# A two-layer trunk on one core: layer 0's first half of the stream kept in SBUF between the MLP and layer 1, mixer weights split 1024 columns at a time

## The chip, the cores and the metric

The kernel runs on one core of a Trainium2 chip. The number that counts is the device time of one execution in microseconds. The core has five engines that each work through their own list of instructions in order, and wait for one another by semaphores: TensorE (PE in the profile; its weight loads are shown apart as PEld), VectorE (DVE), ScalarE (ACT), GpSimd (POOL) and SyncE (SP). SyncE does no arithmetic here: it issues DMA transfers. GpSimd issues some too.

## The reference

The model is a trunk of two residual layers on a stream `x` of 1024 tokens by 1024 features, in float32, with 256 memory tokens beside it.

```python
for layer in range(DEPTH):                       # 2
    h = rms_norm(x, norm_mix[layer])
    if layer == 0:
        y_mix, xq = rglru_group(h, w_in_a, ...)  # gated linear recurrence
    else:
        y_mix, xq = fox_group(h, w_in_b, ...)    # causal attention, 8 heads
    y_mem = memory_group(xq, mem, ...)           # 4 heads onto the memory
    x = x + concatenate([y_mix, y_mem]) @ w_out[layer]
    h = rms_norm(x, norm_mlp[layer])
    x = x + square(relu(h @ w_mlp_in[layer])) @ w_mlp_out[layer]
```

`rms_norm` divides each token by the root of its mean square, so each norm needs sums of squares over all 1024 features of a token. `memory_group` projects the normalised memory tokens by `w_mem_kv` to keys and values, and attends to them with the query `xq`, which comes from the projection of the stream.

## The kernel before

**Layout.** The stream lies transposed, features on partitions: eight feature tiles `k` of 128, in two token halves `h` of 512. A tile 128x512 is 256 KB. Between the stages the stream lives in DRAM, in the array `xspill` (`self.xs`); tiles of it are loaded by `load_x` (L538) into buffers `f`.

**Three matmuls for a product.** Every float32 operand is split into a rounded part and a remainder (`wh` and `wl` for weights, two buffers `r` for activations), and a product is three matmuls: `wh` with both parts of the activation, `wl` with the first. For a weight chunk, `_wpart` (L317 to L320) does this: ScalarE casts (`wh<-wr`, L319), VectorE or GpSimd subtracts (`wl<-wr,wh`, L320). Which engine subtracts a piece is read from `self.pool_parts`, set from the table `TUNE` by stage. A plan of all weight chunks in the order of use says for each in how many pieces it is split; `wr` is loaded by SyncE (L315), three buffers each of `wh` and `wl` go round for most stages, and the next chunks are split as the buffers come free. Chunks that are needed twice are written to DRAM after the split (L343) and loaded back.

**The passage from layer 0's MLP to layer 1.** The MLP runs over eight groups of hidden features (`mlp`). In each, `mlp_z` makes the hidden tiles and `mlp_out` multiplies them by the second weight; both use a scheme of seven products for two token halves and two feature halves, so one product's result is used in two places. In `mlp_out`, `first` copies a product from PSUM (ScalarE, L1075), `then` adds a second product (VectorE, L1080), and `send` (L1220) has GpSimd's queue add the tile to `xspill` by an accumulating DMA. `kv` projects the memory for layer 1: eight weight chunks (`wkv`), taken in pairs, each with 12 matmuls 128x256 into each of two PSUM tiles (L388). In step with it runs `norm_split_back`: for each of the eight feature tiles of the first half it reloads the tile (L538), splits it (ScalarE L488, VectorE L491), squares it (ScalarE L441) and adds the squares up (VectorE L447). Then `xq_proj` multiplies these tiles by `wxqb`.

**The order.** Generators are advanced in a written order; `weave(main, side, rate)` advances the side `rate` steps for each step of the main one. A scheduler with its own time model then orders each engine's list, so the list can differ from the code's order.

**The start.** In layer 0 the tokens are also loaded in a token-major copy (`xtok`), whose squares ScalarE sums (`tok_sums`, L476). `norm_fin_g` makes the reciprocal roots, and where a broadcast over partitions is wanted, GpSimd puts them on a diagonal (L530) and a matmul with ones spreads them (L381, `pso<-f,ones`). For later norms the squares of tiles are summed over partitions by matmuls 128x1 with a constant column (`sq_pe`, `sq_mm`, L465).

## Time and profile before

| | |
|---|---|
| time, median of 3 runs | 2108.54 us (2106.35 to 2111.91) |
| profiled execution, its own time | 2108.65 us |
| its span, first to last instruction | 2106.9 us |
| mean granted TensorE clock | 0.988 |
| TensorE busy | 2055.2 us, 10378 instructions |
| VectorE, ScalarE, GpSimd busy | 1564.0, 1154.3, 463.3 us |
| reloads of `xspill` by SyncE (L538 and others) | 88 of 256 KB |
| accumulating writes to `xspill` by GpSimd | 240 of 256 KB |

A row such as `L320 DVE TENSOR_TENSOR wl<-wr,wh 128x1024 ... x222 | 273.3, 1231 | 172.5 <-ACT wh L319 171.7` reads: line of the kernel, engine, operation, output from inputs, tile shape, count; then busy microseconds and nanoseconds of one; then the microseconds that the engine idled just before these instructions, and what released it. Line numbers are those of the kernel before; in the changed one they are 1 to 23 higher. In a row of waits stand the engine and the line that waited, what it waited for, and the total, the number and the longest of the waits. SPq is SyncE's own queue. Slices of the span are 52.7 us.

### The profile page before, as it was taken

What the parts mean: (1) busy time and instruction counts of PE and PEld (TensorE: products, weight loads), DVE (VectorE), ACT (ScalarE), POOL (GpSimd) and SP (SyncE); (2) the same over time, 40 slices, a digit from 0 to 9 for tenths busy, and PEclk for the clock granted to TensorE, in tenths of its full rate; (3) what the DMA queues carried; (4) which work ended last, traced back from release to release, by engine and by line L of the source; (5) the groups of instructions that cost most, each with busy time, mean ns of one, the idle gap of its engine ahead of it and who ended that gap; (6) DMA issues with size and microseconds to landing.
All of it is one profiled execution on the core that took longest, in us unless ns stands there. A gap on an engine that the chain in (4) does not pass through costs nothing. (4 is left out here: it accounts for less than half of the span.)

```text
span 2106.9 us, 29666 instructions
## 1 busy us (share of the span) xinstructions
PE 2055.2 (98%) x10378; PEld 1712.8 (81%) x10378; DVE 1564.0 (74%) x2916; ACT 1154.3 (55%) x2172; POOL 463.3 (22%) x590
## 2 busy tenths in 40 slices
PE   9999999999999999997999999999999999999999
PEld 7987788888788888876998998777778888888887
DVE  8878698776776776785585778787787768658757
ACT  7756656554554554555464655576554555445544
POOL 1132210201201201214252333232012122022021
PEclk9999999999999999998899999999999999999999
DMA  7433362635635635748568437743446674365374
GB/s 276 151 99 117 101 195 76 130 81 110 131 81 110 135 77 109 160 94 246 192 232 295 151 100 267 239 149 117 145 101 140 139 179 95 80 147 99 78 184 120
DMA packets 122646, 301.56 MB, mean 143 GB/s; under 512 B 13760, under 2 KB 15872, under 8 KB 122496
## 3 DMA queue, kind: packets, MB, share of 16 engines
q1 hardware_dynamic: 79584, 209.41, 29.6%
q0 software_dynamic: 42912, 90.26, 22.8%
q8 instruction: 81, 1.33, 0.3%
q14 instruction: 69, 0.57, 0.1%
HBM read 190.46 MB, written 109.15 MB: 142 GB/s over the span
## 5 line engine op out<-in xcount | busy, mean ns | idle before, releaser
L1064 PE MATMUL pspt<-r,wh 128*128 128x512 f32 x1536 | 491.6, 396 | 1.0 <-ACT wh L319 1.0
L320 DVE TENSOR_TENSOR wl<-wr,wh 128x1024 fp32r<-128x1024 f32 (+2 forms) x354 | 337.9, 965 | 198.0 <-ACT wh L319 196.9
L319 ACT ACTIVATE wh<-wr 128x1024 fp32r<-128x1024 f32 (+3 forms) x403 | 304.5, 777 | 296.4 <-PE pss L1064 73.2
L1220 POOL DMA_DIRECT2D xspill<-f x240 | 212.1, 1111 | 854.8 <-DVE f L1080 825.1
L1064 PEld LDWEIGHTS pspt<-r,wh 128*128 128x128 f32 x1536 | 288.3, 188 | 71.5 <-ACT wh L319 1.4
L1064 PE MATMUL pss<-r,wh 128*128 128x512 f32 x1024 | 329.1, 396 | 0.4 <-DVE r L499 0.4
L1064 PE MATMUL pspt<-r,wl 128*128 128x512 f32 x768 | 304.0, 396 | 0.0
L1064 PE MATMUL pspj<-r,wh 128*128 128x512 f32 x832 | 272.1, 399 | 1.0 <-DVE r L491 1.0
L388 PE MATMUL pspj<-wh,r 128*128 128x256 f32 (+1 forms) x1280 | 252.5, 290 | 15.3 <-ACT r L488 11.7
L499 DVE TENSOR_TENSOR r<-f,r 128x512 fp32r<-128x512 f32 x282 | 191.0, 696 | 75.9 <-DMA xspill<-f 61.3
L1064 PEld LDWEIGHTS pss<-r,wh 128*128 128x128 f32 x1024 | 192.1, 188 | 48.5 <-DVE r L499 0.8
L388 PEld LDWEIGHTS pspj<-wh,r 128*128 128x128 f32 x1280 | 207.1, 194 | 19.7 <-ACT r L488 13.0
L496 ACT ACTIVATE r<-f 128x512 fp32r<-128x512 f32 x282 | 169.6, 625 | 82.8 <-DMA xspill<-f 25.1
L1064 PE MATMUL pss<-r,wl 128*128 128x512 f32 x512 | 202.4, 395 | 0.0
L1064 PEld LDWEIGHTS pspj<-r,wh 128*128 128x128 f32 x832 | 156.6, 189 | 39.8 <-DVE r L491 1.8
L388 PE MATMUL pspj<-wl,r 128*128 128x256 f32 (+1 forms) x640 | 184.9, 289 | 0.2 <-POOL wl L320 0.2
L1064 PEld LDWEIGHTS pspt<-r,wl 128*128 128x128 f32 x768 | 144.5, 188 | 35.2
L1064 PE MATMUL pspj<-r,wl 128*128 128x512 f32 x416 | 164.9, 397 | 0.0
L388 PE MATMUL pspj<-r,wh 128*128 128x512 f32 x480 | 157.8, 404 | 3.9 <-DVE wr L836 1.7
L1085 ACT ACTIVATE f<-f 128x512 f32<-128x512 f32 x128 | 78.8, 626 | 105.1 <-DVE f L1084 102.8
L388 PEld LDWEIGHTS pspj<-wl,r 128*128 128x128 f32 x640 | 123.7, 193 | 1.2 <-POOL wl L320 0.4
L1064 PEld LDWEIGHTS pss<-r,wl 128*128 128x128 f32 x512 | 96.2, 188 | 23.8 <-issue 0.5
(301 smaller groups left out, 3570.2 us busy)
## 6 DMA issues: line engine op xcount, KB each, us to landing
wr<-in_w_dram SPq DMA_DIRECT2D x136, 512.0 KB, 3.9
xspill<-f POOLq DMA_DIRECT2D x240, 256.0 KB, 7.2
f<-xspill SPq DMA_DIRECT2D x88, 256.0 KB, 4.6
xspill<-f SPq DMA_DIRECT2D x48, 256.0 KB, 3.1
wsp<-wh SPq DMA_DIRECT2D x22, 512.0 KB, 5.7
wsp<-wl SPq DMA_DIRECT2D x22, 512.0 KB, 6.1
wh<-wsp POOLq DMA_DIRECT2D x21, 512.0 KB, 5.2
wl<-wsp POOLq DMA_DIRECT2D x21, 512.0 KB, 5.4
```

The lines of the kernel that those rows point to most:

```text
L319: self.wact = self.nc.scalar.activation(hi, raw, AF.Copy)
L320: eng.tensor_tensor(lo, raw, hi.bitcast(F32), ALU.subtract)
L388: self.lastmm = self.nc.tensor.matmul(out, lhsT=a, rhs=b, start=(j == 0), stop=(j == n - 1))
L496: i = self.nc.scalar.activation(hi[:, :n], src, AF.Copy)
L499: self.nc.vector.tensor_tensor(lo[:, :n], src, hi[:, :n].bitcast(F32), ALU.subtract)
L1064: self.lastmm = self.nc.tensor.matmul(ps, lhsT=a, rhs=b, start=(start and c == 0 and j == 0), stop=(c == n - 1 and j == 2), skip_group_che ...
L1085: self.lastsq = self.nc.scalar.activation(f[:, n], f[:, n], AF.Square)
L1220: nc.gpsimd.dma_start(self.xs[2 * q + a, :, b * H:(b + 1) * H], f[:, n], accum_op=ALU.add)
```

## The change

It has five parts.

1. The lists of pieces for GpSimd in `TUNE` are emptied: every weight remainder is VectorE's.
2. The mixer's chunks (`plan_kv`, `plan_mv`, `plan_fox`) are split in one piece of 1024 (or 1056) columns, where it was four. That concerns 41 chunks, of which the first chunk of all keeps its four pieces.
3. The 128x1 matmuls that sum squares before the MLP are taken up later, from hooks in the MLP's first group, and their PSUM bank is taken when the first is done.
4. At the start, `tok_sums` issues all its loads at once; the sums of the second token half stand at the head of `in_g0` and their `norm_fin` at its third step.
5. In layer 0's last MLP group, the first half's eight stream tiles are loaded while the hidden tiles are made. The products for them are added to these tiles on VectorE, the first one too. They are written to `xspill` by plain DMAs of SyncE, and `norm_split_back` takes them from SBUF.

```diff
--- before.py
+++ after.py
@@ -165,11 +165,11 @@
     "cp_kv0": 1,
     "cp_kv1": 0,
     "pa": (),
-    "pb0": (1, 3),
-    "pb1": (0, 1, 2, 3),
-    "pb2": (3,),
+    "pb0": (),
+    "pb1": (),
+    "pb2": (),
     "pm0": (),
-    "pm1": (1, 3),
+    "pm1": (),
 }
 
 
@@ -218,6 +218,7 @@
         self.parked = {}
         self.stp = {}
         self.tst = {}
+        self.xres = {}
         self.xg = [None, None]
         self.ymix = [None, None]
         self.hs = [None, None]
@@ -453,11 +454,12 @@
         if behind is not None:
             self.after(i, behind)
         if m == 0:
-            self.stp[h] = self.psum("o"), []
+            self.stp[h] = [None, []]
         self.stp[h][1].append((m, sq))
-        self.sq_mm(h, 2)
 
     def sq_mm(self, h, keep):
+        if self.stp[h][0] is None:
+            self.stp[h][0] = self.psum("o")
         st, todo = self.stp[h]
         while len(todo) > keep:
             m, sq = todo.pop(0)
@@ -469,15 +471,17 @@
     def tok_sums(self, src, n, tag, behind=None):
         nc = self.nc
         st = self.small(2 * n, tag, 1)
+        xs = [self.F.get() for _ in range(2 * n)]
+        for k, x in enumerate(xs):
+            nc.sync.dma_start(x[:, :H], src[k // 2, :, k % 2 * H:(k % 2 + 1) * H])
         for t in range(n):
             for j in range(2):
-                x = self.F.get()
-                nc.sync.dma_start(x[:, :H], src[t, :, j * H:(j + 1) * H])
+                x = xs[2 * t + j]
                 i = nc.scalar.activation(x[:, :H], x[:, :H], AF.Square, scale=1.0 / math.sqrt(D),
                                          accum_out=st[:, j * n + t:j * n + t + 1])
                 if behind is not None:
                     self.after(i, behind)
-                self.F.put(x)
+        self.F.put(*xs)
         return st
 
     def tok_var(self, v, st, n):
@@ -538,7 +542,7 @@
         self.nc.sync.dma_start(x[:, :H], src[k, :, h * H:(h + 1) * H])
         return x
 
-    def norm_split(self, h, g, src, stats, tok=None):
+    def norm_split(self, h, g, src, stats):
         xs = self.xg[h] = []
         for k in range(8):
             x = self.load_x(k, h, src)
@@ -547,14 +551,12 @@
             xs.append(self.split(x[:, :H], self.pc(g, k)))
             self.F.put(x)
             yield
-        if tok is not None:
-            self.tst[h] = self.tok_sums(tok[4 * h:4 * h + 4], 4, f"tst{h}", self.last_hi)
-
-    def norm_split_back(self, h, g, src):
+
+    def norm_split_back(self, h, g):
         nc = self.nc
         xs = self.xg[h] = [None] * 8
         for j, k in enumerate((0, 2, 4, 6, 1, 3, 5, 7)):
-            x = self.load_x(k, h, src)
+            x = self.xres.pop(k)
             xs[k] = self.split(x[:, :H], self.pc(g, k), behind=self.wact)
             self.sqacc(j, h, x[:, :H], nc.vector, self.last_hi)
             self.F.put(x)
@@ -605,7 +607,7 @@
 
     def plan_kv(self, l, idx=range(8)):
         for c in idx:
-            self.plan.append(self.ent("wkv", l * 8 + c, 1024, 4))
+            self.plan.append(self.ent("wkv", l * 8 + c, 1024, 1))
 
     def kv(self, l):
         nc = self.nc
@@ -792,7 +794,7 @@
 
     def plan_mv(self, name, idx=range(4)):
         for i in idx:
-            self.plan.append(self.ent(name, i, 1024, 4))
+            self.plan.append(self.ent(name, i, 1024, 1))
 
     def proj_T(self, xs, tag="pj"):
         wh, wl = self.wnext()
@@ -1226,7 +1228,20 @@
             nc.sync.dma_start(self.out[2 * q + a, :, b * H:(b + 1) * H], f[:, n])
             self.F.put(f)
 
+        def held(a):
+            def first(q, ps):
+                self.plus(self.xres[2 * q + a], ps)
+
+            def then(q, ps):
+                x = self.xres[2 * q + a]
+                self.plus(x, ps)
+                nc.sync.dma_start(self.xs[2 * q + a, :, :H], x[:, n])
+
+            return first, then
+
         def keep(a, b):
+            if b == 0 and self.xres:
+                return held(a)
             dst = []
 
             def first(q, ps):
@@ -1274,19 +1289,25 @@
         def hook0(key):
             if key in ahead:
                 self.xsplit(ahead[key])
+            if key in ("b11", "b21"):
+                self.sq_mm(1, 6 if key == "b11" else 3)
             if key in ("t2", "t3"):
                 advance(nf)
 
         def hook7(key):
             if key == "t2" and nxt is not None:
                 advance(nxt)
+            if key == "t1" and not l:
+                self.xres = {m: self.load_x(m, 0, self.xs) for m in (0, 2, 4, 6, 1, 3, 5, 7)}
             if key == "t1" and l:
                 self.acc = [self.load_x(2 * q, 0, self.xs) for q in range(4)]
 
         for p in wait:
             for k in ("t3", "t1"):
                 self.xsplit(k)
+            self.sq_mm(1, 5)
             drain(p)
+            self.sq_mm(1, 2)
         for g in range(8):
             if g == 0 and g in self.parked:
                 for k in ("t3", "t1"):
@@ -1326,7 +1347,7 @@
         for w in ("wkb", "wqb"):
             self.plan_mv(w, (2 * c, 2 * c + 1))
         for kk in range(2):
-            self.plan.append(self.ent(f"wvb{c}", kk, 1024 if c else 1056, 4))
+            self.plan.append(self.ent(f"wvb{c}", kk, 1024 if c else 1056, 1))
 
     def fox_proj(self, h, c):
         nc = self.nc
@@ -1591,7 +1612,7 @@
 
 
         xk = self.ins["xtok"]
-        nrm = [self.norm_split_first(0, "gmix0", xT, xk), self.norm_split(1, "gmix0", xT, False, xk)]
+        nrm = [self.norm_split_first(0, "gmix0", xT, xk), self.norm_split(1, "gmix0", xT, False)]
         advance(nrm[0])
         kv = self.kv(0)
 
@@ -1623,7 +1644,10 @@
                     yield
 
         def in_g0():
+            self.tst[1] = self.tok_sums(xk[4:], 4, "tst1", self.wact)
             for m in range(4):
+                if m == 2:
+                    self.norm_fin(1, True)
                 for _ in range(4):
                     advance(kv)
                     yield
@@ -1656,7 +1680,6 @@
         weave(self.xq_proj(0), lru0, TUNE["xq0"])
         drain(lru0)
         self.xg_free(0)
-        self.norm_fin(1, True)
         xa0 = self.xattn(0)
         weave(self.xq_proj(1), xa0, TUNE["xq1"])
         weave(in_u1(), xa0, TUNE["in_u1"])
@@ -1679,8 +1702,8 @@
 
 
         self.fox_setup()
-        advance(kv, 6)
-        weave(kv, self.norm_split_back(0, "gmix1", self.xs), 1.0)
+        advance(kv, 2)
+        weave(kv, self.norm_split_back(0, "gmix1"), 1.0)
         self.vst = {}
         xq = self.xq_proj(0, 1)
         advance(xq, 4)
```

Counted over the whole kernel: remainders of 1024 columns on VectorE go from 222 to 261 (and 2 of 1056), of 256 columns from 112 to 4; on GpSimd 49 remainders go. ScalarE has 38 more casts of 1024 columns (and 2 of 1056), 152 fewer of 256 and 8 fewer of 264, and 8 fewer PSUM copies; VectorE 8 more additions from PSUM. GpSimd issues 232 accumulating DMAs in place of 240, SyncE 56 plain writes to `xspill` in place of 48. The number of matmuls is the same, 10280.

SyncE at the passage from layer 0's MLP to layer 1, where `wxqb` and `wkb` are weights of layer 1's mixer, and `f_...<-xspill` are the first half's stream tiles. Before:

```order
L315 DMA wr_69<-in_wxqb_dram 128x1024
L538 DMA f_894_8484<-xspill 128x512
L315 DMA wr_70<-in_wxqb_dram 128x1024
L538 DMA f_899_8509<-xspill 128x512
L315 DMA wr_71<-in_wxqb_dram 128x1024
L315 DMA wr_72<-in_wxqb_dram 128x1024
L538 DMA f_907_8573<-xspill 128x512
L343 DMA wsp_100<-wh_75 128x1024
L343 DMA wsp_101<-wl_78 128x1024
L315 DMA wr_69<-in_wkb_dram 128x1024
L343 DMA wsp_102<-wh_73 128x1024
L538 DMA f_911_8596<-xspill 128x512
```

With the change, the loads of the tiles, in the list just ahead of the last MLP weights (`w`) and the first of `wkv`:

```order
L542 DMA f_831_7771<-xspill 128x512
L542 DMA f_832_7773<-xspill 128x512
L542 DMA f_833_7775<-xspill 128x512
L542 DMA f_834_7777<-xspill 128x512
L542 DMA f_835_7779<-xspill 128x512
L542 DMA f_836_7781<-xspill 128x512
L542 DMA f_837_7783<-xspill 128x512
L316 DMA wr_69<-in_w_dram 128x1024
L316 DMA wr_71<-in_w_dram 128x1024
L316 DMA wr_72<-in_w_dram 128x1024
L316 DMA wr_70<-in_w_dram 128x1024
L316 DMA wr_69<-in_wkv_dram 128x1024
```

The reloads stood between the weights of the two projections of layer 1; now they stand in a row, ahead of the last four MLP chunks, and in the place of the reloads there are none.

TensorE in the keys and values of layer 1 (`kv`), where a first chunk is `wh_73`, `wl_76`, the second of the pair `wh_74`, `wl_77`, and `pspt` a PSUM tile. Before, at the end of a first chunk:

```order
L388 MATMUL pspt_8670<-wl_76,r_862_8137 128x256
L388 MATMUL pspt_8670<-wh_73,r_863_8138 128x256
L388 MATMUL pspt_8670<-wh_74,r_872_8186 128x256
L388 MATMUL pspt_8670<-wl_77,r_872_8186 128x256
L388 MATMUL pspt_8670<-wh_74,r_873_8187 128x256
L388 MATMUL pspt_8670<-wh_74,r_872_8186 128x256
```

With the change, likewise:

```order
L389 MATMUL pspt_8521<-wl_76,r_862_8049 128x256
L389 MATMUL pspt_8521<-wh_73,r_863_8050 128x256
L389 MATMUL pspt_8521<-wh_74,r_872_8098 128x256
L389 MATMUL pspt_8548<-wh_73,r_856_8001 128x256
L389 MATMUL pspt_8548<-wl_76,r_856_8001 128x256
L389 MATMUL pspt_8548<-wh_73,r_857_8002 128x256
```

and at the end of that chunk's matmuls for the second PSUM tile:

```order
L389 MATMUL pspt_8548<-wh_73,r_862_8049 128x256
L389 MATMUL pspt_8548<-wl_76,r_862_8049 128x256
L389 MATMUL pspt_8548<-wh_73,r_863_8050 128x256
L389 MATMUL pspt_8548<-wh_74,r_872_8098 128x256
L389 MATMUL pspt_8521<-wl_77,r_872_8098 128x256
L389 MATMUL pspt_8521<-wh_74,r_873_8099 128x256
```

Before, the remainder of the second chunk is used by the 14th matmul of a PSUM tile. With the change a second PSUM tile is begun in between, so that it is used by the 27th of the pair.

TensorE at the broadcast of the second token half's roots in layer 0 (`f_...,ones`). Before, it stands in the first query projection (PSUM tiles `pspj` of 128x256):

```order
L388 MATMUL pspj_1929<-wh_75,r_110_1008 128x256
L388 MATMUL pspj_1929<-wl_78,r_110_1008 128x256
L388 MATMUL pspj_1929<-wh_75,r_111_1009 128x256
L381 MATMUL pso_1551<-f_157_1546,ones 128x512
L388 MATMUL pspj_1929<-wh_75,r_113_1071 128x256
L388 MATMUL pspj_1929<-wl_78,r_113_1071 128x256
```

With the change:

```order
L389 MATMUL pspj_1080<-r_11_171,wh_73 128x512
L389 MATMUL pspj_1080<-r_10_170,wl_76 128x512
L382 MATMUL pso_857<-f_105_852,ones 128x512
L389 MATMUL pspj_1080<-r_13_177,wh_73 128x512
L389 MATMUL pspj_1080<-r_14_178,wh_73 128x512
L389 MATMUL pspj_1080<-r_13_177,wl_76 128x512
```

It now stands some 390 matmuls earlier, in the gate projection (128x512).

## The prediction

> **What bounds the kernel now.** I read the page's shares first, then its 40 slices, then the stretch where the slices dip, as a table of windows.
>
> ```profile
> PE 2055.2 (98%) x10378; PEld 1712.8 (81%) x10378; DVE 1564.0 (74%) x2916; ACT 1154.3 (55%) x2172; POOL 463.3 (22%) x590
> PE   9999999999999999997999999999999999999999
> PEclk9999999999999999998899999999999999999999
> ```
>
> TensorE is busy for 98% of the span of 2106.9 us; VectorE for 74%, ScalarE for 55%. Taking work from ScalarE or GpSimd as such is therefore worth nothing: only time in which TensorE idles, or runs at a lower clock, can be won. Slices 18 and 19 (each 52.7 us, so about 950 to 1050) are the only two with a dip in both rows. That is the passage from layer 0's MLP to layer 1's mixer:
>
> ```profile
> 917.50:956.60 39.10, 38.72 (x166) 30.90 (x165) 32.37 (x53) 25.49 (x50) 16.00 (x19) 1.00 0.67 143
> 956.60:983.30 26.70, 24.51 (x199) 23.50 (x198) 17.31 (x37) 16.22 (x45) 13.91 (x16) 1.00 0.83 240
> 983.30:1010.50 27.20, 12.71 (x52) 10.43 (x52) 11.14 (x21) 10.07 (x21) 3.31 (x3) 0.55 0.55 199
> 1010.50:1017.00 6.50, 6.50 (x32) 6.50 (x32) 2.57 (x14) 1.27 (x4) 0.00 (x0) 0.51 0.01 3
> ```
>
> (Columns: stretch, length, then busy time and instructions of PE, PEld, DVE, ACT and POOL, the granted clock, DMA share.) The first is the MLP's end, the second the memory K and V projection of layer 1, in which TensorE loses 2.2 us. In the third, where the memory query projection needs the normalised stream, it is busy 12.71 of 27.20 us for only 52 matmuls, at clock 0.55; in the fourth it is busy throughout, at 0.51. What it waits for stands in the waits from 950 to 1060 (total us, times, longest) and in SyncE's queue from 930 to 1012:
>
> ```profile
> PE pspj L388 <- ACT r L488: 11.7, 4, 5.4
> PE pspt L675 <- DVE r L668: 2.6, 1, 2.6
> ACT r L488 <- DMA f<-xspill: 23.1, 7, 7.1
> SPq L538 <- DVE f L447: 21.9, 5, 7.9
> SPq L538 <- DMA xspill<-f: 8.9, 1, 8.9
> ```
>
> Read backwards: TensorE waits for the cast of a stream tile (L488), the cast waits for the tile's reload from DRAM (seven times, 23.1 us), and the reload on SyncE waits once for the MLP's last accumulating write to land (8.9 us) and five times for the square-add (L447) of an earlier tile, whose buffer it takes. The reloads are a serial loop, one buffer per turn.
>
> **The change part by part.** *Kept tiles (the main term).* The eight reloads and their waits leave that loop: the tiles are fetched during the MLP's last group, get the products added in SBUF, and are there when the projection of K and V begins. At full pace the second stretch does 199 matmuls in 24.51 us, 0.123 us each. By that rate the 52 matmuls of the third take 6.4 us, not 27.2: 20.8 to gain. The fourth at full clock takes 0.51 × 6.50 = 3.3 us: 3.2 to gain. With the 2.2 idle us of the second this is 26.2 us at most.
>
> What is late next is the eight tiles' splitting. These are the durations:
>
> ```profile
> L488 ACT ACTIVATE r<-f,par 128x512 fp32r<-128x512 f32 x56 | 39.7, 717 | 51.0 <-DMA f<-xspill 40.9 <-DVE r L491 4.0 <-DMA f<-in_xT_dram 3.1
> L491 DVE SCALAR_TENSOR_TENSOR r<-f,par,r 128x512 fp32r<-128x512 f32 x56 | 42.6, 764 | 33.9 <-ACT r L488 29.7 <-ACT wh L319 4.0
> L447 DVE TENSOR_TENSOR f<-f,f 128x512 f32<-128x512 f32 x21 | 14.7, 701 | 1.0 <-ACT f L441 0.5 <-DVE fsm L1469 0.4
> L320 DVE TENSOR_TENSOR wl<-wr,wh 128x1024 fp32r<-128x1024 f32 x222 | 273.3, 1231 | 172.5 <-ACT wh L319 171.7 <-issue 0.3
> L319 ACT ACTIVATE wh<-wr 128x1024 fp32r<-128x1024 f32 x223 | 236.1, 1059 | 274.5 <-PE pss L1064 71.7 <-DMA wr<-in_w_dram 67.0 <-PE pspt L1064 53.6
> L1080 DVE TENSOR_TENSOR f<-f,pss 128x512 f32<-128x512 f32 x66 | 44.8, 684 | 9.9 <-PE pspt L1064 6.0 <-PE pss L1064 3.4 <-DMA f<-xspill 0.6
> L1075 ACT ACTIVATE f<-pss 128x512 f32<-128x512 f32 x126 | 74.1, 593 | 46.3 <-PE pss L1064 43.2 <-DMA xspill<-f 3.2
> ```
>
> In the stretch of K and V, VectorE now has 8 × 0.764 (tile remainders) + 7 × 0.701 (square-adds) + 8 × 1.231 (weight remainders) = 20.9 us, and I estimate 4 more for the small steps that it has there today. TensorE needs 24.5 us, so VectorE is just as long: no reserve. Ahead of it, eight first products (0.684 each) go from ScalarE's copies (0.593) to VectorE: 32.37 + 5.5 = 37.9 of 39.1 us in the MLP's last stretch. VectorE enters the K and V stretch full, and each microsecond of backlog may reach TensorE. ScalarE has slack (8 × 0.717 + 8 × 1.059 = 14.2 us and the squares). So some stall stays. Its bounds: 0, if the backlog is worked off under the 199 matmuls, and 11.7 us, if the four waits of today simply have a new releaser. I take 3, nearer the low end, because only the last tile is late by this sum, and the query projection takes the tiles one after the other. Kept: −26.2 + 3 = **−23.2 us**. The eight plain writes on SyncE's queue in place of eight accumulating ones on GpSimd's stand in the order behind loads that are due anyway, and nothing reads that half of the stream before the attention; I cost them at 0 (if they block the weights' loads, rival b).
>
> *Weights in one piece, remainders on VectorE.* Today's quarters:
>
> ```profile
> L319 ACT ACTIVATE wh<-wr 128x256 fp32r<-128x256 f32 x156 | 55.8, 409 | 14.1 <-PE pspj L388 3.2 <-PE pspt L388 2.9 <-DMA wr<-in_wkv_dram 2.1
> L320 DVE TENSOR_TENSOR wl<-wr,wh 128x256 fp32r<-128x256 f32 x112 | 50.1, 476 | 23.9 <-ACT wh L319 23.6
> L320 POOL TENSOR_TENSOR wl<-wr,wh 128x256 fp32r<-128x256 f32 x44 | 40.6, 942 | 72.1 <-ACT wh L319 72.0
> L388 PE MATMUL pspj<-wl,r 128*128 128x256 f32 x576 | 166.6, 289 | 0.2 <-POOL wl L320 0.2
> ACT wh L319 <- PE pspj L388: 13.1, 10, 3.0
> ```
>
> A chunk costs ScalarE 1.059 us in place of 4 × 0.409 = 1.64; over some 40 chunks it saves about 23 us that bind nothing. VectorE takes 39 remainders of 1.231 (48 us) and drops 108 of 0.476 (51 us): nothing. GpSimd drops 44 × 0.942 = 41 us. What can reach TensorE is latency: the first quarter of a chunk is ready 0.409 + 0.476 = 0.89 us after its load, a whole one after 1.059 + 1.231 = 2.29, so 1.4 us later; the last quarter was ready after 4 × 0.409 + 0.476 to 0.942 = 2.1 to 2.6, so no later. Today TensorE loses 0.2 us to such remainders in 576 matmuls, and in the first 235 us ScalarE waits ten times, 13.1 us, for TensorE to free a weight buffer: the weights run ahead. In the changed order of K and V, moreover, a second chunk's remainder is first used by the 27th matmul of a pair of chunks, not by the 14th: TensorE turns to a second PSUM tile in between, and 13 × 0.123 = 1.6 us are more than 1.4. I take **0**; bounds −4 (12 chunks of layer 1's attention, each ready 0.3 us sooner where GpSimd did the last quarter) and +6 for that stage, and more in rival c.
>
> *Start.* The statistics of the second token half move from behind the half's splitting to the head of the gate projection, and their broadcast from behind the first query projection to the gate projection's third step.
>
> ```profile
> ACT f L476 <- DMA f<-in_xtok_dram: 10.2, 7, 2.2
> PE pso L381 <- POOL f L530: 3.1, 1, 3.1
> PE pspj L388 <- ACT f L599: 2.2, 3, 1.2
> ```
>
> The 3.1 us wait of the broadcast for GpSimd's small step goes, since the step lies some 390 matmuls ahead of its old place. Against it, eight loads enter SyncE's queue at once ahead of weight loads. By the longest wait of today a load can come 2.2 us late, twice over at most: bounds −6 (all three waits and 1 us more) and +5. I take **−2.5**.
>
> *Sums over partitions in layers 0 and 1.* The 128×1 matmuls stay as many but are spread over more places. They matter through the clock:
>
> ```profile
> 986.20:1016.90 30.70, 17.96 (x76) 0.50 0.40 144
> 1229.00:1231.90 2.90, 0.93 (x8) 1.00 0.00 0
> 1231.90:1235.30 3.40, 3.40 (x13) 0.50 0.02 5
> 1494.80:1498.20 3.40, 3.40 (x27) 0.99 0.30 110
> 1498.20:1501.60 3.40, 3.40 (x10) 0.50 0.43 154
> ```
>
> (Length, PE busy, clock, DMA share.) At 1231.9 a stretch at half clock follows one in which TensorE idled 2 us of 2.9; at 1498.2 one follows with no idle at all, after a run of 20 sum matmuls. Each costs 1.7 us. A spread run may lose its slow window; two such, so 0 to −3.4, I take **−1.7**. The Trainium skill ("TensorE: Matmul & The Clock Gate", "What's actually happening") gives half rate after at least one idle window of about 3.4 us. By that page the 3 us that I leave at the boundary would cost no clock and these spread runs would win nothing; the trace differs, with 0.50 granted after 2 us of idle and after none.
>
> Sum: −23.2 + 0 − 2.5 − 1.7 = −27.4 us. The profiled execution took 2108.65 us, like the median of the runs, 2108.54: **2081 us**.
>
> **The rivals.** (a) *The wait moves to VectorE.* Its queue, full at 37.9 of 39.1 us, delivers each tile late; the four waits keep their 11.7 us and the clock stays half for two windows (3.4 us). 2081 + 8.7 + 3.4 = 2093. For it: the two sums above have no reserve. Against: the tiles are needed in turn, and the last adds on them follow a product that ends 24 matmuls (by 39.10 us for 166, 5.7 us) ahead of the MLP's end, and they are for the last four of the eight.
>
> (b) *The kept tiles' loads block SyncE.* They stand ahead of four MLP weights and, like today's, must wait until the preceding group's accumulating writes have landed. If one wait of 8.9 us falls there, TensorE stalls for what the buffered weights don't cover, at most 8.9 and one slow window (1.7): 2092. Against: those writes are some 60 us older by then.
>
> (c) *Slower: whole chunks come too late.* If TensorE reaches each chunk just as it is loaded, each of the 41 changed chunks costs the 1.4 us of a later first quarter. From 20 chunks on (28 us) this eats the 27.4; with 22, 2112; with all, 2138. For it: VectorE has the remainders alone now, behind tile work in its queue. Against: 0.2 us of waits today and ScalarE waiting for free buffers.
>
> **How the numbers follow.** Forecast 0.74, (a) 0.12, (b) 0.06, (c) 0.08. The range goes from all bounds that help (no stall 3, start 3.5, clock 1.7, attention 4 to 6: 2081 − 14 = 2067) to the stall at its upper bound with the start's, 2081 + 8.7 + 7.5 = 2097, and a little over for (a): 2100. A difference below 0.3% (6 us) can't be told from none. Faster: the forecast and two thirds of (a) and (b), 0.86; same: the other third, 0.06; slower: (c), 0.08.
>
> **What would show it.** Right: slices 18 and 19 full and at clock 9; no reloads at L538's successor between the K and V and query projections; the cast's wait for `xspill` gone; span near 2079. (a) would show TensorE waiting for VectorE's tile remainder or adds between 950 and 1000; (b) SyncE waiting for `xspill` around 900 and the MLP's matmuls for `wr`; (c) waits of `wh`/`wl` in the projections of layer 1 and the start. I am wrong most simply if the half clock around 986 to 1017 stays though the idle time goes, or if the start or attention shift by more than their bounds.

## The result and the profile after

The changed kernel takes 2084.77 us (median of 4 runs, 2083.12 to 2084.93) against 2108.97 for the kernel before, measured beside it: a ratio of 0.9883, 95% interval 0.9866 to 0.9900. That is 24.2 us less. 2081 was forecast, with a range of 2067 to 2100.

The page of the changed kernel: the busy shares, then TensorE's busy tenths and its granted clock in 40 slices of 52.1 us.

```profile
PE 2048.9 (98%) x10378; PEld 1711.5 (82%) x10378; DVE 1560.1 (75%) x2853; ACT 1138.9 (55%) x2044; POOL 411.8 (20%) x533
PE   8999999999999999999999999989999999999999
PEclk9999999999999999999999999999899999999999
```

The dip at slices 18 and 19 is gone from both rows. TensorE's share is 98% in both by rounding: its idle time falls from 51.7 to 34.3 us, and its busy time by 6.3, since work at half clock counts as busy for twice as long. What is left are small dips in the first slice, in slice 26 (around 1380 us) and, in the clock, in slice 28 (around 1485).

The passage from layer 0's MLP to layer 1, in windows with the columns of those before (busy time and count of PE, PEld, DVE, ACT, POOL; clock; DMA share):

```profile
905.70:936.40 30.70, 27.60 (x109) 21.22 (x109) 29.07 (x47) 14.21 (x23) 0.00 (x0) 0.94 0.21 69
936.40:957.00 20.60, 20.60 (x91) 16.64 (x90) 14.10 (x20) 9.82 (x16) 5.71 (x7) 1.00 0.73 202
957.00:987.10 30.10, 30.10 (x258) 30.10 (x257) 26.79 (x52) 23.66 (x42) 1.13 (x2) 1.00 0.85 255
```

The third row is the memory's keys and values and the query projection together: 258 matmuls in 30.10 us, TensorE never idle, clock 1.00. Before, the same work took from 956.6 to beyond 1010. VectorE is busy for 26.79 of these 30.10 us, near full as forecast, and still ahead of TensorE: the last tile's remainder is done at 983.0 us, as TensorE nears the end of the projection and the sum over partitions that follows it. Two rows of the timeline (start, duration):

```profile
982.24 0.75 DVE L495 SCALAR_TENSOR_TENSOR r<-f,par,r 128x512 fp32r<-128x512 f32 x1
984.98 0.95 PE L382 MATMUL pso<-cD,f 128*128 128x1 f32 x8
```

The first row of the windows shows what was not foreseen at that place: in the MLP's end TensorE is idle for 3.1 of 30.7 us, at a mean clock of 0.94, and VectorE is busy for 29.07.

To see where time went over the whole span, the two traces can be laid side by side by TensorE's own work: its matmuls (10378 in every trace) are summed up by their columns, and the two times at which the same sum is reached are compared. The table gives the change of that difference over each stretch, in us, for one profiled execution of each kernel (stretches by the times of the kernel before, the whole up to the last matmul; the runs in the lower lines come below). The matmuls' sum is the same in all kernels but their order differs a little, so some tenths are rounding.

| kernel | start, 0 to 375 | MLP's end, 916 to 941 | passage, 941 to 1040 | attention, 1040 to 1585 | whole |
|---|---|---|---|---|---|
| changed | -4.7 | +5.0 | -27.8 | +3.8 | -23.8 |
| kept tiles alone | -0.7 | +5.7 | -27.2 | +7.7 | -14.1 |
| all but the kept tiles | -5.7 | 0.0 | -1.4 | +8.1 | +1.2 |
| weights alone | +9.6 | 0.0 | -2.1 | +4.9 | +12.6 |
| start alone | -0.3 | 0.0 | -1.0 | +5.1 | +3.6 |
| 128x1 sums alone | -1.3 | 0.0 | -1.3 | 0.0 | -2.1 |
| changed, sums as before | -3.6 | +5.8 | -27.8 | +8.0 | -17.5 |
| changed, pieces as before | -5.4 | +5.0 | -27.2 | +1.7 | -25.8 |
| changed, first product copied | -4.6 | +1.0 | -27.8 | +5.4 | -25.8 |
| changed, attention in pieces | -6.5 | +5.0 | -27.6 | +4.7 | -24.5 |
| copied, and all in pieces | -4.1 | +1.0 | -25.2 | +7.3 | -21.1 |
| copied, and attention in pieces | -3.1 | +1.0 | -27.6 | +0.4 | -29.0 |
| before, reloads ahead | +2.2 | 0.0 | -18.6 | +0.2 | -16.0 |

Two columns repeat within a microsecond wherever the same part is in, the passage and the MLP's end, with one exception: the passage of the kernel with the copies and all pieces gains 25.2 us and not 27 to 28. The attention's column does not repeat. It holds most of the slow-clock windows, and executions of one kernel differ by more than the numbers in it (all but the kept tiles: ten runs from 2102.6 to 2113.0), so a single number there says little.

### The profile page after: what moved, and what is told of

It reads as the page before. It is cut to its first block, busy times and chain, and to the rows that moved or that the text cites. A ratio compares the mean times of both kernels' runs of the same rounds, so it can differ in the third digit from the quotient of the medians.

```text
span 2083.2 us, 29289 instructions
## 1 busy us (share of the span) xinstructions
PE 2048.9 (98%) x10378; PEld 1711.5 (82%) x10378; DVE 1560.1 (75%) x2853; ACT 1138.9 (55%) x2044; POOL 411.8 (20%) x533
## 4 chain that ended last, share of the span: by engine, by line
PE 82%; DVE 8%; issue 4%; DMA 4%; ACT 2%; POOL 1%; SPq 0%; DVEq 0%; ACTq 0%; POOLq 0%
PE pspt L1066 24%; PE pss L1066 16%; PE pspj L1066 13%; PE pspj L389 13%; PE pso L1066 3%; PE pspt L389 2%; PE pss L1477 1%; PE pss L389 1%; DVE wl L321 1%; PE pspt L1519 1%; PE pss L382 1%; DMA f<-xspill 1%; DMA f<-in_xT_dram 1%; DMA xspill<-f 1%; PE pspj L978 1%
## 5 line engine op out<-in xcount | busy, mean ns | idle before, releaser
L320 ACT ACTIVATE wh<-wr 128x1024 fp32r<-128x1024 f32 (+2 forms) x283 | 289.4, 1024 | 296.3 <-PE pss L1066 79.8
L1222 POOL DMA_DIRECT2D xspill<-f x232 | 202.8, 1092 | 874.9 <-DVE f L1082 832.2
L389 PE MATMUL pspj<-wh,r 128*128 128x256 f32 (+1 forms) x1280 | 244.8, 285 | 3.1 <-DMA wh<-wsp 1.5
L389 PEld LDWEIGHTS pspj<-wh,r 128*128 128x128 f32 x1280 | 201.8, 189 | 5.1 <-DMA wh<-wsp 1.6
```

The lines of the kernel that those rows point to most:

```text
L320: self.wact = self.nc.scalar.activation(hi, raw, AF.Copy)
L389: self.lastmm = self.nc.tensor.matmul(out, lhsT=a, rhs=b, start=(j == 0), stop=(j == n - 1))
L1222: nc.gpsimd.dma_start(self.xs[2 * q + a, :, b * H:(b + 1) * H], f[:, n], accum_op=ALU.add)
```

## The experiments

**Kept tiles alone** (`held_only`). The kernel before with part 5 only:

```diff
+                self.xres = {m: self.load_x(m, 0, self.xs) for m in (0, 2, 4, 6, 1, 3, 5, 7)}
...
+            if b == 0 and self.xres:
+                return held(a)
...
-            x = self.load_x(k, h, src)
+            x = self.xres.pop(k)
...
-        advance(kv, 6)
+        advance(kv, 2)
...
```

> The kernel before with the kept tiles alone (part 5). Theory: the passage gains 27 to 28 us, as in the changed kernel, and VectorE at the MLP's end is less full, since half of each key and value chunk's remainders is still GpSimd's: a stall of 0 to 2 us in place of 5. Time about 2082 to 2085 against 2109, the start unchanged. Rival (the passage gains because the weights come in one piece and leave ScalarE and VectorE to the tiles): less than half of the gain, 2095 to 2103.

Measured: 2094.5 us, ratio 0.9929 (0.9914 to 0.9944). The passage gains its 27.2 us without any other part, so the rival's cause falls. But three expectations were wrong. The time misses the 2082 to 2085 and lies just below the rival's range. The MLP's end loses 5.7 us, no less than in the changed kernel, although half of each key and value chunk was GpSimd's: those chunks are not what fills VectorE there. And the attention was 7.7 us longer in this execution, with 23.8 us of half clock between 1190 and 1560 where the kernel before had 13.6; half of the difference is 5.1 us.

**All but the kept tiles** (`all_but_held`).

```diff
-            if b == 0 and self.xres:
-                return held(a)
...
-            x = self.xres.pop(k)
+            x = self.load_x(k, h, src)
...
-        advance(kv, 2)
+        advance(kv, 6)
...
```

> The changed kernel with the reloads of before (all parts but 5). Theory: the passage still loses about 25 us, the start wins 4.7, the attention loses some 4: 2105 to 2111. Rival (weights in one piece free the passage): 2085 to 2095.

Measured: 2107.62 us, ratio 0.9990 (0.9979 to 1.0000). As the theory had it, though the attention lost 8.1 us and not 4. With the run before, this shows part 5 as the cause of the gain in the passage. Part 5 also begins the keys and values in another order (`advance(kv, 2)` for 6), which was not tried apart.

**Weights alone** (`weights_only`).

(Here and below, the lines of `TUNE` are drawn together into one.)

```diff
-    "pb0": (1, 3), "pb1": (0, 1, 2, 3), "pb2": (3,), "pm1": (1, 3),
+    "pb0": (), "pb1": (), "pb2": (), "pm1": (),
...
-            self.plan.append(self.ent("wkv", l * 8 + c, 1024, 4))
+            self.plan.append(self.ent("wkv", l * 8 + c, 1024, 1))
...
```

> The kernel before with chunks in one piece and all remainders on VectorE (parts 1 and 2). Theory: nothing that can be told from no change, 2106 to 2113: the start and the passage as before, the attention 0 to 4 us longer. Rival (whole chunks come 1.4 us late at about half of the 41 changed chunks): 2130 or more, with waits for wl in the projections. Rival (freed ScalarE and GpSimd gain): 2095 to 2102.

Measured: 2119.01 us, ratio 1.0047 (1.0028 to 1.0066). Slower, between theory and rival. TensorE's waits for a weight's remainder in the projections of L388 over the whole span, and three windows of TensorE alone (length, busy, clock, DMA share):

```profile
PE pspj L388 <- DVE wl L320: 3.5, 4, 1.3
```

```profile
165.00:167.30 2.30, 0.67 (x3) 1.00 0.00 0
167.30:174.10 6.80, 5.87 (x15) 0.50 0.27 77
320.90:331.10 10.20, 10.20 (x33) 0.50 0.48 154
```

Whole chunks do come late, by 1.3 us at the longest (1.4 was worked out), but not at half of 41. Of the four waits two, 1.26 us at 128.5 and 1.03 at 1088.3, are for chunks that this edit made whole; the other two are for chunks of `wina`, which were in one piece before too. The larger share of the 9.6 us that the start loses is clock: these two stretches are 17.0 us at half, where the kernel before has one of 3.4 in the start. Half of the difference, 6.8 us, is an estimate of what that costs. The first follows 1.6 idle us of 2.3.

**Start alone** (`start_only`).

```diff
+        xs = [self.F.get() for _ in range(2 * n)]
+        for k, x in enumerate(xs):
+            nc.sync.dma_start(x[:, :H], src[k // 2, :, k % 2 * H:(k % 2 + 1) * H])
...
+            self.tst[1] = self.tok_sums(xk[4:], 4, "tst1", self.wact)
             for m in range(4):
+                if m == 2:
+                    self.norm_fin(1, True)
...
-        self.norm_fin(1, True)
```

> The kernel before with the token sums moved at the start (part 4). Theory: the first 350 us win 3 to 5 us, of which the later slow-clock window at 314 us is no part: 2104 to 2106. Rival (the start wins by the weights in one piece): 2108 to 2111.

Measured: 2107.41 us, ratio 0.9987 (0.9978 to 0.9997). The stretch from 129 to 244 us is 7.5 us shorter, as in every kernel with this part. The one before it is 1.9 us longer, and the slow window near 312 is longer (below). The times alone show a gain of 3 us, with an interval that nearly touches none; the median lies between the two texts.

The stretch before 129 us holds two effects. It is 0.5 to 1.9 us longer in the three kernels with this part and the start's chunks in pieces, 2.5 to 5.4 in the six with this part and whole chunks there, and 3.4 with the weights alone. By these numbers some 2 to 3 us of the loss there go with the whole chunks, an estimate.

**128x1 sums alone** (`sums_only`).

```diff
-        self.sq_mm(h, 2)
...
+            if key in ("b11", "b21"):
+                self.sq_mm(1, 6 if key == "b11" else 3)
...
+            self.sq_mm(1, 5)
             drain(p)
+            self.sq_mm(1, 2)
...
```

> The kernel before with the 128x1 sums taken up later (part 3) alone. Theory (a run of 128x1 matmuls brings half clock by itself, a shorter one does not): the window at 314 us goes, 1.7 us; of those at 1498 and 1512 one may go: 2105 to 2108 against 2109 to 2110, hardly to be told from none. Rival (the windows follow idle time and the phase of the meter): the windows of the profile stay or move, 2107 to 2112.

**Changed kernel with the sums as before** (`sums_as_before`): the same lines taken back out of the changed kernel.

> The changed kernel with the 128x1 sums where they were (all parts but 3). Theory: a half clock window of 3.4 to 10.2 us comes back around 310 us, as the two kernels with the sums in their old place and another part changed show it: 2 to 5 us, 2086 to 2090. Rival: the window around 310 us does not hang on the sums: 2083 to 2086.

Measured: 2108.97 us, ratio 0.9993 (0.9982 to 1.0005) for the sums alone, and 2089.22 us, 0.9901 (0.9883 to 0.9920) for the changed kernel without them, 4.5 us more than the changed kernel, with overlapping intervals. The first lies in the range of its rival, the second in that of its theory. The totals cannot tell, but the place can. First the start alone, which has the sums in their old place (a row of its timeline, and two windows of TensorE):

```profile
307.68 2.73 PE L465 MATMUL pso<-cD,f 128*128 128x1 f32 x24
```

```profile
300.00:311.70 11.70, 11.70 (x62) 1.00 0.66 213
311.70:321.90 10.20, 10.20 (x33) 0.50 0.28 93
```

and the sums alone:

```profile
315.14 1.62 PE L466 MATMUL pso<-cD,f 128*128 128x1 f32 x14
```

```profile
313.00:320.00 7.00, 7.00 (x45) 1.00 0.65 210
```

A run of 24 sum matmuls is followed by 10.2 us at clock 0.50, with TensorE busy for all of the 11.7 us ahead. A run of 14 is followed by full clock. In each of the six profiles with the sums in their old place, 24 such matmuls stand there in a row or with a break of 0.2 us, and a half-clock stretch of 3.4 to 10.2 us begins within 1.3 us of their end. None of the eight with the sums spread has one there. In layer 1, where the changed order leaves a run of 24 and the old one a run of 32, this does not hold as firmly: half clock begins within 1 us of the end of the run in five of eight kernels with 24 and in five of six with 32, and not in the other four, the changed kernel among them.

**Pieces as before** (`pieces_as_before`): the changed kernel without parts 1 and 2.

```diff
-    "pb0": (), "pb1": (), "pb2": (), "pm1": (),
+    "pb0": (1, 3), "pb1": (0, 1, 2, 3), "pb2": (3,), "pm1": (1, 3),
...
-            self.plan.append(self.ent("wkv", l * 8 + c, 1024, 1))
+            self.plan.append(self.ent("wkv", l * 8 + c, 1024, 4))
...
```

> The changed kernel with chunks in four pieces and GpSimd's share as before (all parts but 1 and 2). Theory, after the run in which these two parts alone cost 9 us: they cost here too, mostly at the start: 2076 to 2081. Rival (with the start's order changed, the whole chunks are no longer late, and the parts are needed for that order): 2084 to 2090.

Measured: 2083.65 us, ratio 0.9875 (0.9859 to 0.9892), not to be told from the changed kernel's 0.9883. The time lies just below the rival's range, and neither text is borne out in full: with the start's order changed, whole chunks no longer cost 9 us, and they win nothing either.

**First product copied** (`copy_first`).

```diff
-            def first(q, ps):
-                self.plus(self.xres[2 * q + a], ps)
+            dst = []
+            first = self.copies(dst)
             def then(q, ps):
                 x = self.xres[2 * q + a]
-                self.plus(x, ps)
+                self.plus(dst[q], ps)
+                nc.gpsimd.tensor_tensor(x[:, n], x[:, n], dst[q][:, n], ALU.add)
...
```

> The changed kernel, but a kept tile's first product is copied from PSUM by ScalarE as before, the second is added to the copy on VectorE, and GpSimd adds the sum to the kept tile. Theory (VectorE, full at the MLP's end, frees PSUM late, and the eight added steps are what fills it): the 5 us at the MLP's last products go, the passage stays as it is (at most 2 us longer, since GpSimd's addition comes before a tile's split): 2079 to 2082 against 2084.8. Rival (the stall there is the wait for the last group's weights, or for the tiles' loads): no change.

Measured: 2083.59 us, ratio 0.9876 (0.9855 to 0.9896). The place answers again. In the changed kernel, the waits from 895 to 940 us, the timeline of the stall, and the windows of TensorE at it:

```profile
PE pspt L1066 <- DVE f L1082: 2.9, 2, 2.3
```

```profile
925.56 0.67 DVE L1082 TENSOR_TENSOR f<-f,pspt 128x512 f32<-128x512 f32 x1
...
926.38 0.47 PE L1066 MATMUL pspt<-r,wh 128*128 128x512 f32 x1 [2.26 <-DVE f L1082]
926.76 1.27 DVE L1082 TENSOR_TENSOR f<-f,pspt 128x512 f32<-128x512 f32 x2
...
927.49 1.09 PE L1066 MATMUL pspt<-r,wh 128*128 128x512 f32 x2 [0.64 <-DVE f L1082]
```

```profile
925.50:928.90 3.40, 1.68 (x4) 1.00 0.40 151
928.90:932.30 3.40, 3.40 (x9) 0.51 0.52 173
```

TensorE waits for a PSUM tile that VectorE has yet to add up and release; VectorE is busy without a break up to there, as three more windows show (its time is the third pair, 25.0 us of 25):

```profile
905.00:912.00 7.00, 7.00 (x31) 5.63 (x31) 7.00 (x11) 3.37 (x6) 0.27 (x1) 1.00 0.00 0
912.00:924.00 12.00, 12.00 (x52) 9.41 (x51) 12.00 (x21) 8.01 (x14) 0.00 (x0) 1.00 0.06 8
924.00:930.00 6.00, 2.90 (x8) 1.59 (x8) 6.00 (x11) 2.52 (x6) 0.00 (x0) 0.91 0.54 205
```

VectorE had no gap there in the kernel before either, and TensorE did not wait:

```profile
911.00:923.00 12.00, 12.00 (x53) 9.67 (x52) 12.00 (x19) 8.01 (x13) 0.00 (x0) 1.00 0.01 1
923.00:929.00 6.00, 6.00 (x27) 4.56 (x25) 6.00 (x11) 5.87 (x12) 0.00 (x0) 1.00 0.29 90
```

So the stretch without a gap does not make the stall by itself. Steps that are added in it can only push back those behind them, and those release PSUM.

At the stall, half of 3.4 us idle is followed by 3.4 us at half clock. With the first products as copies on ScalarE, the only wait of TensorE at this place is

```profile
925.05 0.50 PE L1066 MATMUL pss<-r,wh 128*128 128x512 f32 x1 [0.42 <-DVE r L503]
```

with no slow window, and the stretch loses 1.0 us in place of 5.0, while the passage keeps its 27.8. VectorE is still busy without a break from 915 to 930 us there. So it was the added steps on VectorE. In the total the 4 us are not seen, and the time misses the 2079 to 2082 of the theory: 1.2 us between the medians, with intervals that overlap.

**Reloads ahead** (`reload_ahead`): the kernel before, with an edit of two lines that parts the buffers from the way through DRAM.

```diff
+        xt = {k: self.load_x(k, h, src) for k in (0, 2, 4, 6, 1, 3, 5, 7)}
         for j, k in enumerate((0, 2, 4, 6, 1, 3, 5, 7)):
-            x = self.load_x(k, h, src)
+            x = xt[k]
```

> The kernel before, with the eight reloads of the first half issued together into eight buffers ahead of the splits, and the accumulating writes as they were. It takes the serial loop of buffers away and leaves the way through DRAM. Theory that the loop is the loss (five waits of a reload for the square-add of an earlier tile): the passage gains most of its 27 us and the MLP's end stays free of a stall, 2082 to 2090 against 2110. Rival that the way through DRAM is the loss (the reload waits for the last accumulating writes, 8.9 us at longest): the passage gains less than 12 us, 2098 to 2108.

Measured: 2091.39 us, ratio 0.9913 (0.9890 to 0.9935): 1.4 us above the theory's range, with 18.6 of the passage's 27.8 us. The waits of SyncE's queue, 930 to 1012 us:

```profile
SPq L538 <- DMA xspill<-f: 27.5, 8, 10.7
```

No reload waits for a square-add any more; each of the eight now waits for an accumulating write. So two thirds of the loss was the serial use of buffers. The rest, 9 us, goes only with part 5. TensorE still waits 4.0 us in this passage, in six waits, mostly for VectorE's steps, and has one half-clock window of 3.4 us. The late writes are the likely source of that, but the way through DRAM and the order of the keys and values were not tried apart. This edit does about as well in total as the kept tiles alone, since it loses nothing at the MLP's end (0.0 against 5.7 us) and, in these executions, less in the attention (0.2 against 7.7).

**Attention in pieces** (`attention_pieces`): the changed kernel with the attention's chunks alone as before.

```diff
-    "pb1": (), "pb2": (),
+    "pb1": (0, 1, 2, 3), "pb2": (3,),
...
-            self.plan_mv(w, (2 * c, 2 * c + 1))
+            self.plan_mv(w, (2 * c, 2 * c + 1), 4)
-            self.plan.append(self.ent(f"wvb{c}", kk, 1024 if c else 1056, 1))
+            self.plan.append(self.ent(f"wvb{c}", kk, 1024 if c else 1056, 4))
...
```

> The changed kernel with the attention's twelve chunks in four pieces and GpSimd's share of them as before. Theory (the 5 us that the five kernels with whole chunks lose in the stretch of some 50 us around 1350 come from these chunks): that stretch is as before, the 2 us won ahead of it go too, and the time is 2080 to 2084 against 2084.8. Rival (the order of the attention is just drawn anew by each edit): the stretch stays 4 to 5 us longer.

Measured: 2084.32 us, ratio 0.9879 (0.9864 to 0.9895). The stretch that reaches from 1365 to 1413 us in the kernel before is 4.3 to 6.9 us longer in the five kernels with whole chunks in the attention, and between 0.5 shorter and 1.7 longer in the eight others, this one among them (0.4). So the chunks' form shows at this place. The changed kernel's waits of TensorE in it are mostly for the softmax's maxima and for a copy, not for weights:

```profile
PE pss L1477 <- DVE mn L1482: 1.8, 2, 1.4
PE pspj L1066 <- ACT f L1077: 1.5, 1, 1.5
```

In this kernel the total came out the same, since in the profiled execution the stretches around it lost as much. How the whole chunks delay those maxima was not followed further.

**Both edits** (`kept_by_copy`: the copies, and all chunks in pieces; `copy_and_pieces`: the copies, and the attention's chunks in pieces).

```diff
+            first = self.copies(dst)
...
+                nc.gpsimd.tensor_tensor(x[:, n], x[:, n], dst[q][:, n], ALU.add)
...
+    "pb1": (0, 1, 2, 3), "pb2": (3,),
...
```

> Kept tiles with the first product copied by ScalarE and added by GpSimd, the start's order and the 128x1 sums as in the changed kernel, chunks in four pieces as before. Theory (the stall of 5 us at the MLP's end and the whole chunks' waits both go): 2077 to 2081, the fastest of all. Rival (the two gains do not add, since each edit draws the order anew): 2082 to 2086.

> The changed kernel with both single edits: the kept tiles' first product by ScalarE's copy and GpSimd's addition, and the attention's twelve chunks in four pieces with GpSimd's share. Theory: the MLP's end loses 1 us in place of 5, the stretch around 1350 is as before, and the slow windows of the attention eat a part: 2078 to 2082, the lowest. Rival (what is won ahead of the attention is given back in its slow windows, as with the earlier pair of edits): 2082 to 2085.

Measured: 2082.47 us, 0.9866 (0.9850 to 0.9883), and 2083.69 us, 0.9883 (0.9867 to 0.9900). The profiled execution of the second was the shortest of all, 2080.04 us, but its other runs reach 2085.69. Neither can be told from the changed kernel; the rivals hold for the times, and no version here beats the changed kernel clearly.

## Why the prediction was right, step by step

The forecast was 27.4 us and 24.2 came (2108.65 to 2084.88 in the profiled executions, 23.8). The sum is near partly by luck: terms of both signs were missed, and they cancel. By place, the profiled executions differ by -27.8 in the passage, +5.0 at the MLP's end, -4.7 in the start and +3.8 in the attention.

- **Kept tiles**: -23.2 forecast, -27.8 measured in the passage, and the runs with this part alone and without it show it to be this part's. With the 5.0 us that it costs at the MLP's end (next point) its net is -22.8, so the term is near for a reason that the prediction did not have. The mechanism in the passage was right. Mis-sized were the residual stall, 3 us, which did not come there, and the pace: 0.123 us a matmul was taken from a stretch that three waits break up, and around a wait the busy time holds a whole matmul of 0.28 to 0.38 us; undisturbed ones start 0.118 us apart in both kernels, and the changed kernel does 258 in 30.10, 0.117. The reading of the chain (reloads as a serial loop) was right for two thirds; of the last third, the runs show only that it goes with part 5.
- **VectorE full** was the right warning at the wrong place. The prediction worked out 37.9 of 39.1 us for the MLP's last stretch and let the backlog reach the passage (rival a). VectorE works it off there, but inside the MLP its delay holds PSUM tiles that TensorE needs: +5.0 us, of which 1.7 are one half-clock window. That term was missing: the prediction's 32.37 of 39.1 us hid that VectorE had no gap at all from 911 to 929 us before the change, where the added steps then went.
- **SyncE** (rival b): the kept tiles' loads did wait for accumulating writes, in five waits, and the cast of a last MLP weight waited 9.5 us for its load behind them. TensorE waited for none of it; the weights in the buffers covered it. The rows are of 860 to 925 us.

```profile
SPq L542 <- DMA xspill<-f: 9.3, 5, 3.4
ACT wh L320 <- DMA wr<-in_w_dram: 9.5, 1, 9.5
```

- **Weights in one piece**: 0 forecast. The changed kernel waits for remainders, in these rows of the whole span,

```profile
PE pspj L389 <- DVE wl L321: 3.6, 3, 1.3
PE pspt L1066 <- DVE wl L321: 1.3, 2, 1.1
PE pspt L389 <- DVE wl L321: 1.2, 1, 1.2
```

6.1 us in six waits, none longer than the 1.4 us worked out. Three of them, 3.6 us at 48.5, 118.5 and 1052.8 us, are for chunks that the change made whole; the others are for a chunk of `wina` and for MLP weights, which were in one piece before too. With the pieces as before, the kernel waits 0.6 us for remainders at the same places. So rival c's mechanism is real, but at three places in place of 41. That these parts cost nothing holds only beside the others: alone they made the kernel 0.5% slower. The prediction's parts do not add up one by one, and it treated them as if they did.
- **Start**: -2.5 forecast without the clock; about -3.0 measured (-4.7 less some 1.7, half of the slow window). The 7.5 us won from 129 to 244 us were more than the waits that were counted, and 4.2 us were lost ahead of 129, of which some 2 to 3 go with the whole chunks. By that the start's own gain is an estimated 5 to 6 us, twice the forecast, and the near hit is luck too.
- **128x1 sums**: -1.7 forecast for one of two windows, at 1231.9 and 1498.2 us. Neither was won: layer 1 of the changed kernel has one at 1205.4 and one of 13.7 us at 1481.9. The window at 314 us, which the prediction did not show, went, some 1.7 us; the size was right by luck. From 1040 to 1585 us half clock grew from 13.6 to 23.9 us, and half of the difference, 5.1 us, is more than the 3.8 lost in the attention, a term that the sum did not have. The longest of these windows, and the stretch ahead of it:

```profile
1480.00:1481.90 1.90, 0.73 (x2) 1.00 0.38 115
1481.90:1495.60 13.70, 12.53 (x37) 0.50 0.33 119
```

On the clock, the trace goes on differing from the rule of the Trainium skill ("TensorE: Matmul & The Clock Gate", "What's actually happening"), by which half rate comes after at least one idle window of about 3.4 us: at 925.5 a window with 1.7 us of idle sufficed, and after runs of 24 sum matmuls in the start none was needed.

## What to carry to other kernels

A reload that waits for the previous tile's last reader is a serial loop however early it stands in the list. Count its buffers first: here an edit of two lines with eight buffers gave two thirds of what keeping the tiles gave in the passage, at no cost to VectorE. Before moving work to an engine, look for the stretch in which it has no gap already rather than at its mean, and ask which PSUM tile it will then release late. And judge parts of a change at their own place in the trace: effects of 5 us repeated within one there, while the totals could not tell them apart.

## What the runs showed of the hardware that was not expected

In these traces TensorE's clock falls to half after work as well as after idleness. In the start, runs of 24 matmuls of 128x1, 2.73 us without a gap or 3.0 with one of 0.2, were followed by 3.4 to 10.2 us at clock 0.50, where runs of 14 to 18 were not; by half of their length, these windows cost 1.7 to 5.1 us.

What waits and such runs have in common can be read from the 14 traces, though no run was made to test it. All half-clock windows of a trace begin on one grid with steps of 3.41 us. Add up the columns of the matmuls that start in a step; the median is 7216. Of 8221 steps at full clock with at least 3100 columns, none is followed by half clock; of 45 with fewer than 2500, 44 are; of the 55 between, 28. A wait lowers the sum, and so does a run of 24 matmuls of one column when most of it falls into one step: in the six kernels with the sums in their old place, 17 to 21 of them do, and 2580 to 3090 columns are left. The four runs in layer 1 after which no half clock came were split by the grid (15 and 9 in the changed kernel), and every step kept at least 3599 columns.

The windows last whole steps, 3.4 us or a multiple. The clock explains only a part of the spread between executions: over the 47 runs of the kernel before that were taken beside the experiments, the mean granted clock goes from 0.984 to 0.991, and its correlation with the time is -0.46, which is about a fifth of the variance.
